# The last feed-forward's output projection by seven block products instead of eight, its modulation tiles moved one feed-forward ahead

## The chip, the cores and the metric

One NeuronCore of a Trainium2 chip runs the whole program in one launch. The metric is the device time of that launch in microseconds (us). The kernel before takes 2341.85 us, the median of three runs (2340.1 to 2344.75).

## The reference

The model is one inference step of a small diffusion backbone: 128 prompt tokens and 512 latent tokens of width 1024 go through two layers. Each layer has a feed-forward, a mixer and a second feed-forward, each with its own shift, scale and gate from a modulation vector. What the change touches is the feed-forward and the modulation:

```python
def ada(cvec, w_mod, b_mod):
    m = jax.nn.silu(cvec) @ w_mod + b_mod          # 9 vectors of 1024: shift, scale, gate three times
    ...
def ffn_sub(x, g, shift, scale, gate, w_in, w_out):
    h = modulate(rms_norm(x, g), shift, scale)
    a, b = jnp.split(h @ w_in, 2, axis=-1)          # 1024 -> 2 x 2816
    return x + gate * (FFN_RESIDUAL * ((jax.nn.silu(a) * b) @ w_out))   # 2816 -> 1024
```

All data are float32. The 2816 inner features are 22 tiles of 128, the 1024 outputs are 8 tiles of 128, and the 640 tokens are two groups of 320.

## The kernel before, in words

**Layout.** Features lie on the 128 partitions and tokens on the free axis. `x` is 8 tiles of 128 x 640. Group 0 holds tokens 0 to 319, all latent; group 1 holds 192 latent and 128 prompt tokens, which have different modulation, so an update of group 1 is two instructions (192 and 128 columns).

**Split operands.** TensorE runs on float32r. Every operand is cut into a high part (ScalarE copies it to float32r, `whi` at L104, `hid` at L583) and a low part (VectorE subtracts, `wlo` at L105, `hid` at L584). A product of two operands is three matmuls: high with high, high with low, low with high. Each matmul has 320 columns.

**A feed-forward** (`ffn`) works through its 22 inner tiles `f`. For each `f` an in-projection makes the tile of `silu(a) * b`, called hidden, which is then split. The first four or five tiles are made with plain products (`in_one`, `start4`). From then on `product_set` (L516) makes the two 1024-deep products of a tile for both token groups as a 2 x 2 block problem with seven block products instead of eight (Strassen's scheme in Winograd's form): VectorE forms sums and differences of the weight halves (L522, L525 to L527), TensorE runs seven products of 12 matmuls each (L126), and ScalarE copies a finished partial sum from one PSUM bank into another (`seeded`, L535) so that the next product accumulates onto it.

**The out-projection** follows in chunks of inner tiles, `CHUNKS = (6, 6, 5, 5)` (L19). A chunk starts when one more hidden tile than it needs is made. For each of the 8 output tiles `m` one weight unit is loaded and split, `mm3` (L128) runs three matmuls for each inner tile and group (L134, L135, L137), and `gate_add` (L400) adds the gated result to `x`. The last chunk goes by halves of four output tiles, each with both groups, and accumulates the squares for the next norm (L294, L298) on its way. In the last feed-forward the final norm (`rstd`, L318, and `final`, L354) and the stores of `yT` follow.

**Modulation.** Layer 0's first vectors are made with TensorE at the start. All later ones are made on VectorE while the feed-forwards run: `mod_tile` (L154) loads a 128 x 1024 piece of the transposed modulation weight into a `raw` buffer and runs two multiply-and-reduce instructions (L159, one per condition vector). `filler` hands such tiles out: four early ones, some spread over the in-projections from `f = 7` on (`spread`, L561), and one after each output tile of the first three chunks. A feed-forward with any of them first loads and activates the condition vectors (`mod_load`, L146). The third feed-forward (layer 1, first) has 36 such tiles, the last one has 4 (L1457, L1462).

**Buffers and order.** Weights come through one DMA queue of SyncE into a ring of 4 `raw` tiles, split weights lie in rings of 5 (`whi`, `wlo`), hidden tiles in a ring of 7, and there are 8 PSUM banks. Every engine runs its own queue in order; a scheduler of the framework lays down that order when the program is built. An instruction whose operand is not ready holds all that stand behind it on its engine.

Of the kernel before, what the change touches and what calls it, by code (L numbers as in the profile page):

```python
# [17 lines left out]
NFT = 22  # L18
CHUNKS = (6, 6, 5, 5)  # L19
# [21 lines left out]
class Body:  # L41
# [58 lines left out]
    def split_w(self, r, n=1024):  # L100
        nc = self.nc
        hi = self.wr.tile([P, 1024], F32R, tag="whi", name=self.nm("whi"))
        lo = self.wr.tile([P, 1024], F32R, tag="wlo", name=self.nm("wlo"))
        a = (nc.scalar.activation(hi[:, :n], r[:, :n], AF.Copy),  # L104
             nc.vector.tensor_tensor(lo[:, :n], r[:, :n], hi[:, :n].bitcast(F32), op=ALU.subtract))  # L105
# [449 lines left out]
    def ffn(self, ctx, l, j, nxt, fill=(), first=False):  # L555
# [3 lines left out]
        nconv = NCONV[2 * l + j]  # L559
        early = 4  # L560
# [9 lines left out]
        def hidden(pa, pb):  # L570
# [7 lines left out]
            return hid_split(sl)  # L578

        def hid_split(sl):  # L580
# [6 lines left out]
        def hidden7(x, z, q, y, w5):  # L587
# [7 lines left out]
            return hid_split(sl)  # L595
# [19 lines left out]
        if first:  # L615
            hid = [hidden(p3[0], p3[1])]
            hid.append(hidden(p3[2], in_one(self.unit(win[l, j, 1, 1]))))
        else:
            self.h_blocks(hp)
            p4 = self.start4([win[l, j, f, ab] for f in range(2) for ab in range(2)], hf=(l, 2 * j))  # L620
            hid = [hidden(p4[0], p4[1]), hidden(p4[2], p4[3])]
# [5 lines left out]
        while len(hid) < nconv:  # L627
# [8 lines left out]
            hid.append(hidden(*p))  # L636
# [4 lines left out]
        def inproj(f):  # L641
            hid.append(hidden7(*self.product_set([win[l, j, f, ab] for ab in range(2)])))
            fill_set(f)

        f0 = 0
        for c, n in enumerate(CHUNKS):
            last = c == len(CHUNKS) - 1
# [5 lines left out]
            if not last:  # L653
# [788 lines left out]
def body(nc, tc, i, o):  # L1442
    with ExitStack() as ctx:
# [73 lines left out]
def layout(a):  # L1517
# [15 lines left out]
    parts, f0 = [], 0  # L1533
    for n in CHUNKS:
        w = a["w_ffn_out"][:, :, f0 * P:(f0 + n) * P].reshape(2, 2, n, P, KT, P)
        parts.append(w.transpose(0, 1, 4, 3, 2, 5).reshape(2, 2, -1))
        f0 += n
    d["w_out"] = np.concatenate(parts, 2)
# [54 lines left out]
```

## Time and profile before

| | |
|---|---|
| median of 3 runs | 2341.85 us |
| profiled execution, its own time | 2340.22 us |
| span of its instructions | 2338.4 us |
| TensorE busy | 2292.8 us, 98% |
| VectorE busy | 1900.8 us, 81% |
| ScalarE busy | 1124.5 us, 48% |
| mean granted TensorE clock | 0.997 of full |

The span runs from the first to the last instruction; the execution's own time is 1.8 us more. The views used below are the page's summary, the chain of work that ended last, lists of who waited for whom, groups of instructions, the DMA list, timelines of one engine and tables of busy time for chosen stretches. In a timeline row stand start, duration, engine, line, operation, output<-input, shapes, and in brackets the idle time before it with what ended it. The last feed-forward fills the stretch from about 1888 us to the end; its first product set starts at 1949.11 us.

### The profile page before, as it was taken

To read this page: it belongs to the slowest core of one execution; us is meant where nothing else is said; L and a number is where in the kernel's file an instruction comes from. 1 tells how busy PE (TensorE), PEld (TensorE's weight loads), DVE (VectorE), ACT (ScalarE), POOL (GpSimd) and SP (SyncE) were. 2 spreads that over 40 slices of the span, in tenths; PEclk is the share of its full clock that TensorE was granted. 3 is DMA by queue.
4 is the path that set the end of the run, shared out by engine and by line. 5 is a ranking of instruction groups with operands and counts; after the bars stand their busy time and mean duration, and the time that the engine had idled before them with its cause. 6 is when DMAs were issued, how large, how long until landed. Compare 5 with 4: busy or idle time off the path is not lost.

```text
span 2338.4 us, 40528 instructions
## 1 busy us (share of the span) xinstructions
PE 2292.8 (98%) x15949; PEld 2220.1 (95%) x15950; DVE 1900.8 (81%) x3779; ACT 1124.5 (48%) x2066; POOL 2.2 (0%) x10
## 2 busy tenths in 40 slices
PE   9999999999999999999999999999999999999998
PEld 6999999998889999999999999998888899999997
DVE  6999989795889989787888888969878798565665
ACT  5535253463666434334552525347756674252442
POOL 0000000000000000000000000000000000000000
PEclk9999999999999999999999999999999999999999
DMA  7353544332111535343234343422100013222221
GB/s 295 118 189 125 192 136 162 111 108 89 47 48 64 169 111 162 100 155 126 82 113 160 108 159 113 147 94 79 42 29 28 28 54 122 78 90 75 89 72 64
DMA packets 81230, 253.31 MB, mean 108 GB/s; under 512 B 9616, under 2 KB 15632, under 8 KB 81040
## 3 DMA queue, kind: packets, MB, share of 16 engines
q1 hardware_dynamic: 81040, 250.72, 32.4%
q8 instruction: 126, 2.06, 0.4%
q14 instruction: 64, 0.52, 0.1%
HBM read 247.28 MB, written 3.41 MB: 107 GB/s over the span
## 4 chain that ended last, share of the span: by engine, by line
PE 87%; DVE 7%; ACT 2%; DMA 2%; issue 1%; SPq 0%; DVEq 0%; ACTq 0%
PE mm L126 34%; PE mm L134 15%; PE mm L135 15%; PE mm L137 15%; PE tr L730 2%; PE pv L1368 2%; PE sc L1333 1%; DVE wlo L105 1%; DMA rawm<-in_wmT 1%; PE pv L1133 1%; DVE t L298 1%; DVE x L400 1%; DVE s L1337 1%; PE mm L881 0%; DVE junk L159 0%
## 5 line engine op out<-in xcount | busy, mean ns | idle before, releaser
L104 ACT ACTIVATE whi<-raw 128x1024 fp32r<-128x1024 f32 (+2 forms) x419 | 407.2, 978 | 564.9 <-PE mm L135 255.5
L105 DVE TENSOR_TENSOR wlo<-raw,whi 128x1024 fp32r<-128x1024 f32 (+2 forms) x419 | 465.6, 1116 | 113.1 <-ACT whi L104 112.6
L134 PE MATMUL mm<-hid,whi 128*128 128x320 f32 x1408 | 427.3, 310 | 0.0
L135 PE MATMUL mm<-hid,whi 128*128 128x320 f32 x1408 | 425.7, 308 | 0.0
L126 PE MATMUL mm<-hhi,whi 128*128 128x320 f32 x1136 | 351.0, 309 | 0.0
L126 PE MATMUL mm<-hhi,wlo 128*128 128x320 f32 x1136 | 350.8, 309 | 0.0
L126 PE MATMUL mm<-hlo,whi 128*128 128x320 f32 x1136 | 350.4, 308 | 0.0
L137 PE MATMUL mm<-hid,wlo 128*128 128x320 f32 x1408 | 346.2, 309 | 0.0
L159 DVE CUSTOM_DVE_ANT_0 junk<-rawm,sil 128x1024 bf16<-128x1024 f32 x256 | 312.0, 1219 | 22.5 <-DMA rawm<-in_wmT 17.6
L400 DVE SCALAR_TENSOR_TENSOR x<-mm,mod,x 128x192 f32<-128x192 f32 (+2 forms) x576 | 226.2, 433 | 114.0 <-PE mm L137 112.7
L134 PE MATMUL mm<-hhi,whi 128*128 128x320 f32 x896 | 276.3, 320 | 6.2 <-ACT hhi L345 5.6
L135 PE MATMUL mm<-hlo,whi 128*128 128x320 f32 x896 | 274.9, 312 | 0.7 <-DVE hlo L348 0.6
L135 PEld LDWEIGHTS mm<-hid,whi 128*128 128x128 f32 x1408 | 264.3, 188 | 0.8
L134 PEld LDWEIGHTS mm<-hid,whi 128*128 128x128 f32 x1408 | 264.3, 188 | 0.8
L137 PE MATMUL mm<-hhi,wlo 128*128 128x320 f32 x896 | 247.9, 311 | 2.8 <-DVE wlo L105 2.8
L137 PEld LDWEIGHTS mm<-hid,wlo 128*128 128x128 f32 x1408 | 241.4, 188 | 0.0
L126 PEld LDWEIGHTS mm<-hhi,whi 128*128 128x128 f32 x1136 | 213.2, 188 | 0.1
L126 PEld LDWEIGHTS mm<-hlo,whi 128*128 128x128 f32 x1136 | 213.3, 188 | 0.0
L126 PEld LDWEIGHTS mm<-hhi,wlo 128*128 128x128 f32 x1136 | 213.2, 188 | 0.0
L134 PEld LDWEIGHTS mm<-hhi,whi 128*128 128x128 f32 x896 | 167.3, 189 | 15.0 <-ACT hhi L345 8.7
L126 PE MATMUL mm<-Th,whi 128*128 128x320 f32 x568 | 175.7, 309 | 3.0 <-ACT mm L535 3.0
L126 PE MATMUL mm<-Tl,whi 128*128 128x320 f32 x568 | 175.2, 308 | 0.0
(229 smaller groups left out, 4094.6 us busy)
## 6 DMA issues: line engine op xcount, KB each, us to landing
raw<-in_w_in SPq DMA_DIRECT2D x176, 512.0 KB, 3.8
rawm<-in_wmT SPq DMA_DIRECT2D x128, 512.0 KB, 3.7
raw<-in_w_out SPq DMA_DIRECT2D x64, 384.0 KB, 3.5
raw<-in_w_out SPq DMA_DIRECT2D x64, 320.0 KB, 3.0
wm<-in_wm SPq DMA_DIRECT2D x16, 512.0 KB, 10.2
raw<-in_w_ab SPq DMA_DIRECT2D x12, 512.0 KB, 4.2
raw<-in_w_c SPq DMA_DIRECT2D x10, 512.0 KB, 3.6
sil<-in_c SPq DMA_DIRECT2D x8, 512.0 KB, 4.8
```

The lines of the kernel that those rows point to most:

```text
L104: a = (nc.scalar.activation(hi[:, :n], r[:, :n], AF.Copy), nc.vector.tensor_tensor(lo[:, :n], r[:, :n], hi[:, :n].bitcast(F32), op=ALU.sub ...
L105: nc.vector.tensor_tensor(lo[:, :n], r[:, :n], hi[:, :n].bitcast(F32), op=ALU.subtract))
L126: nc.tensor.matmul(out, a[:, c], b, start=start and first, stop=last, skip_group_check=True)
L134: nc.tensor.matmul(out, hi[:, c], rh, start=start, stop=False)
L135: nc.tensor.matmul(out, hi[:, c], rl, start=False, stop=False)
L137: nc.tensor.matmul(out, lo[:, c], rh, start=False, stop=stop)
L159: nc.vector.tensor_tensor_reduce(out=self.junk, in0=r, in1=self.sil[:, q], op0=ALU.mult, op1=ALU.add, scale=1.0, scalar=0.0, accum_out=sel ...
L298: t = nc.vector.tensor_tensor(a, a, sq, op=ALU.add)
L400: a = nc.vector.scalar_tensor_tensor(out=x[:, c], in0=ps[:, c], scalar=self.mod[:, q, l, v, m:m + 1], in1=x[:, c], op0=ALU.mult, op1=ALU.add)
L730: self.nc.tensor.transpose(ps[:, a * P:(a + 1) * P], src[:, b * P:(b + 1) * P], self.ident)
L1133: nc.tensor.matmul(st["pv"][64 * f:64 * f + 64, ti * P:(ti + 1) * P], V[:, sl, vc[f]], st[ti, f][:, a * P:(a + 1) * P], start=a == 0, stop ...
L1368: nc.tensor.matmul(st["pv"][64 * f:64 * f + 64, ti * P:(ti + 1) * P], V[:, (4, 0, 1, 2, 3)[a], vc], rhs, start=a == 0, stop=a == 4)
```

## The change

Only the last feed-forward (layer 1, second) computes its out-projection differently.

- Its chunks become 4, 4, 4, 4 and 6 inner tiles. The chunks of four use a new function `out_set`; the last chunk of six keeps the old form.
- `out_set` makes two output tiles at a time. The four inner tiles, as two halves of two, the two output tiles and the two token groups are a 2 x 2 block problem, done with seven products of 6 matmuls (L690 in the new program) instead of eight. VectorE forms four 128 x 256 combinations of the two weight tiles (L676 to L679). Three of the products need combinations of hidden tiles.
- `hid_split` prepares those: of the first two tiles of a chunk only group 0 is split (`hk`, a new ring of three), and the rest is kept unsplit until the tile two places on is there; then three differences are taken (L599 to L601) and three full splits are made instead of one.
- The four sets of a chunk are interleaved in the code: four steps of one set alternate with the first three of the next.
- The four modulation tiles of the last feed-forward move into the third, which then has 40; `mod_begin` and the loading of the condition vectors drop out of the last.
- The output weight is laid out to match; for the other three feed-forwards the chunks stay.

```diff
-CHUNKS = (6, 6, 5, 5)
+CHUNKS = ((6, 6, 5, 5),) * 3 + ((4, 4, 4, 4, 6),)
+SEVEN = 3
...
-        def hid_split(sl):
+        def hid_split(sl, f):
+            if not seven or f >= NFT - chunks[-1]:
+                return split_full(sl)
+            k = f % 4
+            b11, b12 = grp(sl, 0), grp(sl, 1)
+            if k < 2:
+                half = hp.tile([P, 2, G], F32R, tag="hk", bufs=3, name=self.nm("hk"))
+                nc.scalar.activation(half[:, 0], b11, AF.Copy)
+                nc.vector.tensor_tensor(half[:, 1], b11, half[:, 0].bitcast(F32), op=ALU.subtract)
+                nc.vector.tensor_tensor(b11, b12, b11, op=ALU.subtract)
+                kept[f] = sl
+                return half[:, 0], half[:, 1]
+            h2 = split_full(sl)
+            t = kept.pop(f - 2)
+            t1, t3, t4, t2 = grp(t, 0), grp(t, 1), b11, b12
+            nc.vector.tensor_tensor(t3, b12, t3, op=ALU.subtract)
+            nc.vector.tensor_tensor(t2, b12, t1, op=ALU.subtract)
+            nc.vector.tensor_tensor(t4, b11, t2, op=ALU.subtract)
+            pairs[f] = h2, split_full(t), split_full(sl)
+            return h2
...
+        def out_set(wa, wb, m, f0):
+            half = lambda t, a, b=None: t[:, 256 * a:256 * (a + 1 if b is None else b)]
+            r, s = (self.raw.tile([P, 1024], F32, tag="raw", name=self.nm("raw")) for _ in range(2))
+            nc.sync.dma_start(out=half(r, 0, 2), in_=wb)
+            nc.sync.dma_start(out=half(r, 2, 4), in_=wa)
+            nc.vector.tensor_tensor(half(s, 0), half(r, 0), half(r, 1), op=ALU.add)
+            nc.vector.tensor_tensor(half(s, 1), half(s, 0), half(r, 2), op=ALU.subtract)
+            nc.vector.tensor_tensor(half(s, 2), half(r, 2), half(r, 0), op=ALU.subtract)
+            nc.vector.tensor_tensor(half(s, 3), half(r, 3), half(s, 1), op=ALU.subtract)
+            wr = self.split_w(r, slice(256, 1024))
+            ws = self.split_w(s)
...
+            x = self.bank()[:, :G]
+            product(x, wr, 2, h1, True)
+            yield
+            w = self.bank()[:, :G]
+            product(w, ws, 0, side(t13, 0), True)
+            y = seeded(x)
+            w5 = self.g()
+            nc.scalar.activation(w5, w, AF.Copy)
+            yield
+            product(y, ws, 1, side(t42, 1), False)
+            z = seeded(y)
+            yield
+            product(x, wr, 3, side(hh, 0), False)
+            self.gate_add(m, 0, x, l, v)
+            yield
+            product(y, ws, 2, side(t13, 1), False)
+            q = seeded(y)
+            t = self.g()
+            nc.vector.tensor_tensor(t, y, w5, op=ALU.add)
+            self.gate_add(m + 1, 1, t, l, v)
+            yield
+            product(z, ws, 3, side(hh, 1), False)
+            nc.vector.tensor_tensor(w5, z, w5, op=ALU.add)
+            self.gate_add(m, 1, w5, l, v)
+            yield
+            product(q, wr, 1, side(t42, 0), False)
+            self.gate_add(m + 1, 0, q, l, v)
+            yield
...
+            if seven and not last:
+                behind = None
+                for m in range(0, KT, 2):
+                    step = out_set(wc[m], wc[m + 1], m, f0)
+                    for k in range(3):
+                        if behind:
+                            next(behind)
+                        next(step)
+                    if behind:
+                        next(behind)
+                    behind = step
+                for _ in behind:
+                    pass
...
-            b.ffn(c, 1, 0, (1, 1), vf(1, range(4, 9))[:36])
+            b.ffn(c, 1, 0, (1, 1), vf(1, range(4, 9)))
...
-            b.mod_begin(c)
-            b.ffn(c, 1, 1, None, vf(1, range(4, 9))[36:])
+            b.ffn(c, 1, 1, None)
```

Three places show how the queues look. The numbers in the names tell tiles apart. In the new program the line numbers are a little higher: its L107 is the old L105 (`wlo`), its L402 the old L400 (`gate_add`), its L524, L527 to L529 the old L522, L525 to L527, its L161 the old L159.

The first is VectorE in the out-projection's first chunk of the last feed-forward. Before, it stood so (two output tiles):

```order
L400 SCALAR_TENSOR_TENSOR x_70<-mm_22123,mod,x_70 128x320
L400 SCALAR_TENSOR_TENSOR x_70<-mm_22124,mod,x_70 128x192
L400 SCALAR_TENSOR_TENSOR x_70<-mm_22124,mod,x_70 128x128
L105 TENSOR_TENSOR wlo_22355<-raw_22352,whi_22354 128x768
L400 SCALAR_TENSOR_TENSOR x_71<-mm_22170,mod,x_71 128x320
L400 SCALAR_TENSOR_TENSOR x_71<-mm_22171,mod,x_71 128x192
L400 SCALAR_TENSOR_TENSOR x_71<-mm_22171,mod,x_71 128x128
L105 TENSOR_TENSOR wlo_22402<-raw_22399,whi_22401 128x768
```

Now a stretch of it reads as follows; `wlo_22009` and `wlo_22082`, just ahead of it, belong to the third and the fourth set of the chunk, and `raw_22180` is a weight of the next in-projection.

```order
L715 TENSOR_TENSOR g_22027<-mm_21961,g_21963 128x320
L402 SCALAR_TENSOR_TENSOR x_73<-g_22027,mod,x_73 128x192
L402 SCALAR_TENSOR_TENSOR x_73<-g_22027,mod,x_73 128x128
L524 TENSOR_TENSOR s_3632_22182<-raw_22180 128x512
L719 TENSOR_TENSOR g_21963<-mm_21980,g_21963 128x320
L527 TENSOR_TENSOR raw_22180<-raw_22178,raw_22180 128x512
L402 SCALAR_TENSOR_TENSOR x_72<-g_21963,mod,x_72 128x192
L402 SCALAR_TENSOR_TENSOR x_72<-g_21963,mod,x_72 128x128
L402 SCALAR_TENSOR_TENSOR x_73<-mm_22025,mod,x_73 128x320
L107 TENSOR_TENSOR wlo_22086<-raw_22074,whi_22085 128x1024
```

The last row is the low part of the fourth set's combined weights. It now stands behind two instructions (L524, L527) that read the next in-projection's weight.

The second is TensorE in the same chunk. Before, the first rows of one output tile (its first inner tile, both groups):

```order
L134 MATMUL mm_22217<-hid_21429,whi_22213 128x320
L135 MATMUL mm_22217<-hid_21429,whi_22213 128x320
L134 MATMUL mm_22218<-hid_21429,whi_22213 128x320
L135 MATMUL mm_22218<-hid_21429,whi_22213 128x320
L137 MATMUL mm_22217<-hid_21429,wlo_22214 128x320
L137 MATMUL mm_22218<-hid_21429,wlo_22214 128x320
```

Now, where the fourth set's second product begins (`mm_22108`, weights `whi_22085` and `wlo_22086`), between the first matmul of the third set's sixth product (`mm_22057`) and the rest of it:

```order
L690 MATMUL mm_22057<-hid_21585,whi_22008 128x320
L690 MATMUL mm_22108<-hid_21591,whi_22085 128x320 x2
L690 MATMUL mm_22108<-hid_21591,wlo_22086 128x320
L690 MATMUL mm_22108<-hid_21725,whi_22085 128x320 x2
L690 MATMUL mm_22108<-hid_21725,wlo_22086 128x320
L690 MATMUL mm_22057<-hid_21585,whi_22008 128x320
```

The matmul on `wlo_22086` is the third of its product; all products behind it on TensorE wait with it.

The third is VectorE in the third feed-forward, at the in-projection of `f = 7`. Before:

```order
L525 TENSOR_TENSOR raw_14189<-raw_14187,raw_14189 128x512
L105 TENSOR_TENSOR wlo_14075<-raw_14055,whi_14074 128x1024
L590 TENSOR_TENSOR g_14043<-mm_14000,g_14002 128x320
L592 TENSOR_TENSOR g_14002<-mm_13974,g_14002 128x320
L105 TENSOR_TENSOR wlo_14194<-raw_14187,whi_14193 128x1024
```

Now:

```order
L527 TENSOR_TENSOR raw_14189<-raw_14187,raw_14189 128x512
L161 ISA junk,mod<-rawm_14317,sil 128x1024
L161 ISA mod 128x1
L161 ISA junk,mod<-rawm_14317,sil 128x1024
L161 ISA mod 128x1
L107 TENSOR_TENSOR wlo_14075<-raw_14055,whi_14074 128x1024
L615 TENSOR_TENSOR g_14043<-mm_14000,g_14002 128x320
```

One modulation tile (two multiply-and-reduce instructions, each with a read of its sum) has been put ahead of a weight split; three more stand further on.

More of the change, by code (lines that the diff above doesn't have):

```diff
@@ L559, in ffn @@
         nconv = NCONV[2 * l + j]
+        chunks, seven = CHUNKS[2 * l + j], 2 * l + j == SEVEN
+        pairs, kept = {}, {}
         early = 4
@@ L568, in ffn, with hidden @@
         v = 2 + 6 * j
-        def hidden(pa, pb):
+        def hidden(f, pa, pb):
             sl = self.t()
@@ L585, in hid_split, with hidden7 @@
             return hi, lo
-        def hidden7(x, z, q, y, w5):
+        def hidden7(f, x, z, q, y, w5):
             sl, t = self.t(), self.g()
@@ L615, in ffn @@
         if first:
-            hid = [hidden(p3[0], p3[1])]
-            hid.append(hidden(p3[2], in_one(self.unit(win[l, j, 1, 1]))))
+            hid = [hidden(0, p3[0], p3[1])]
+            hid.append(hidden(1, p3[2], in_one(self.unit(win[l, j, 1, 1]))))
         else:
@@ L620, in ffn @@
             p4 = self.start4([win[l, j, f, ab] for f in range(2) for ab in range(2)], hf=(l, 2 * j))
-            hid = [hidden(p4[0], p4[1]), hidden(p4[2], p4[3])]
+            hid = [hidden(f, p4[2 * f], p4[2 * f + 1]) for f in range(2)]
         if fill:
@@ L635, in ffn @@
                 p.append(in_one(w))
-            hid.append(hidden(*p))
+            hid.append(hidden(len(hid), *p))
         for _ in sums:
@@ L641, in inproj, with product, seeded @@
         def inproj(f):
-            hid.append(hidden7(*self.product_set([win[l, j, f, ab] for ab in range(2)])))
+            hid.append(hidden7(f, *self.product_set([win[l, j, f, ab] for ab in range(2)])))
             fill_set(f)
+        def out_set(wa, wb, m, f0):
[9 more added lines that the diff above has]
+            ws = self.split_w(s)
+            h1 = [hid[f0 + k] for k in range(2)]
+            hh, t13, t42 = zip(*(pairs[f0 + k] for k in (2, 3)))
+            side = lambda t, g: [(grp(a, g), grp(b, g)) for a, b in t]
+            def product(p, w, j, rs, start):
+                for k, (rh, rl) in enumerate(rs):
+                    c = slice((2 * j + k) * P, (2 * j + k + 1) * P)
+                    for a, b, first, last in ((w[0], rh, k == 0, False), (w[0], rl, False, False), (w[1], rh, False, k == 1)):
+                        nc.tensor.matmul(p, a[:, c], b, start=start and first, stop=last, skip_group_check=True)
+            def seeded(src):
+                p = self.bank()[:, :G]
+                nc.scalar.activation(p, src, AF.Copy)
+                return p
+            x = self.bank()[:, :G]
[26 more added lines that the diff above has]
+            yield
@@ L645, in ffn @@
         f0 = 0
-        for c, n in enumerate(CHUNKS):
-            last = c == len(CHUNKS) - 1
+        for c, n in enumerate(chunks):
+            last = c == len(chunks) - 1
             while len(hid) < min(NFT, f0 + n + 1):
@@ L652, in ffn @@
             hk = lambda k, g: (grp(ht[k][0], g), grp(ht[k][1], g))
-            if not last:
+            if seven and not last:
[11 more added lines that the diff above has]
+                    pass
+            elif not last:
                 for m in range(KT):
```

23 lines of the change are left out of this document (13 added, 10 removed).

## The prediction, made before the changed kernel was run

> **What bounds the kernel now.** I read the page's summary first, then for the stretch that changes the chain that ended last, TensorE's waits and the tables of busy time.
>
> ```profile
> PE 2292.8 (98%) x15949; PEld 2220.1 (95%) x15950; DVE 1900.8 (81%) x3779; ACT 1124.5 (48%) x2066; POOL 2.2 (0%) x10
> 1949.11 36.92 PE mm L126 x252
> 2028.27 73.83 PE mm L126 x504
> 2144.35 61.53 PE mm L126 x420
> 2241.07 49.22 PE mm L126 x336
> ```
>
> The last four rows are the chain's long pieces in the last feed-forward: uninterrupted TensorE work, at 73.83 / 504 = 0.1465 us for each 320-column matmul. One in-projection (84 matmuls) is 12.3 us.
>
> ```profile
> PE mm L137 <- DVE wlo L105: 0.4, 1, 0.4
> 1929.20:1987.60 58.40, 58.40 (x400) 58.40 (x399) 47.38 (x75) 27.55 (x46) 0.00 (x0) 1.00 0.38 122
> 1987.60:2104.60 117.00, 117.00 (x801) 117.00 (x800) 73.20 (x112) 47.31 (x75) 0.00 (x0) 1.00 0.25 84
> 2104.60:2280.00 175.40, 175.40 (x1198) 175.40 (x1198) 109.66 (x174) 67.87 (x106) 0.00 (x0) 1.00 0.24 79
> ```
>
> The first row is TensorE's only wait from 1899 to 2322 us. The others give, after the length of the stretch, busy time of TensorE, its weight loads, VectorE and ScalarE. TensorE is never idle, the granted clock is 1.00, and VectorE is busy 73.20 of 117.00 us, 63%. So a matmul taken out of this stretch is 0.1465 us off the end, as long as VectorE can feed the new form.
>
> **Removed: 96 matmuls.** Plain, 22 inner tiles x 8 output tiles x 2 groups x 3 = 1056 matmuls. Now 4 chunks x 4 sets x 7 products x 6 = 672, and the last chunk 6 x 8 x 2 x 3 = 288: 960. The gain is 96 x 0.1465 = **14.06 us**. It is on the path, since nothing else ended last there.
>
> **Moved: four modulation tiles.** Each is one 512 KB load and two L159 instructions.
>
> ```profile
> L159 DVE CUSTOM_DVE_ANT_0 junk<-rawm,sil 128x1024 bf16<-128x1024 f32 x256 | 312.0, 1219 | 22.5 <-DMA rawm<-in_wmT 17.6
> 1220.00:1280.00 60.00, 58.92 (x402) 58.66 (x402) 53.93 (x96) 18.39 (x27) 0.00 (x0) 1.00 0.54 178
> 1340.00:1400.00 60.00, 60.00 (x411) 60.00 (x410) 52.54 (x93) 17.70 (x25) 0.00 (x0) 1.00 0.53 169
> PE mm L126 <- ACT mm L535: 1.4, 2, 1.1
> ```
>
> That is 2 x 1.22 = 2.4 us of VectorE each, in in-projections of 12.3 us in the third feed-forward, where VectorE has about 7 us in 60 free (rows two and three) and DMA is busy half the time. Twelve of fifteen in-projections carry one such tile instead of eight. I cost it at nothing, because TensorE's work covers it. The bound from above is the first feed-forward, which spreads 20 tiles over the same fifteen in-projections: the last row is TensorE's whole wait there from 100 to 470 us, 1.4 us. So 0 to 1.4 us. In the last feed-forward the four tiles with their loads, the two loads of condition vectors and their activation go from a stretch in which TensorE never waited, so nothing is gained on the path; but eight L159 instructions (9.8 us of VectorE's 47.38 in the first table row) make room for what follows.
>
> **Added: VectorE work.** Prices come from neighbours in its timeline:
>
> ```profile
> 2036.34 1.23 DVE L105 TENSOR_TENSOR wlo<-raw,whi 128x1024 fp32r<-128x1024 f32 x1 [1.85 <-ACT whi L104]
> 2038.85 0.49 DVE L590 TENSOR_TENSOR g<-mm,g 128x320 f32<-128x320 f32 x1 [1.29 <-PE mm L126]
> 2039.45 0.49 DVE L592 TENSOR_TENSOR g<-mm,g 128x320 f32<-128x320 f32 x1
> 2039.86 1.22 DVE L105 TENSOR_TENSOR wlo<-raw,whi 128x1024 fp32r<-128x1024 f32 x1
> 2040.99 0.48 DVE L593 TENSOR_TENSOR t<-t,mm 128x320 f32<-128x320 f32 x1
> 2041.39 0.48 DVE L594 TENSOR_TENSOR t<-t,g 128x320 f32<-128x320 f32 x1
> 2041.79 0.68 DVE L526 TENSOR_TENSOR raw<-s,raw 128x512 f32<-128x512 f32 x1
> 2042.51 0.69 DVE L527 TENSOR_TENSOR raw<-raw 128x512 f32<-128x512 f32 x1
> 2043.11 0.82 DVE L584 TENSOR_TENSOR hid<-t,hid 128x640 fp32r<-128x640 f32 x1
> 2101.39 0.95 DVE L105 TENSOR_TENSOR wlo<-raw,whi 128x768 fp32r<-128x768 f32 x1
> 2102.26 0.48 DVE L593 TENSOR_TENSOR t<-t,mm 128x320 f32<-128x320 f32 x1
> 1991.21 1.14 DVE L400 SCALAR_TENSOR_TENSOR x<-mm,mod,x 128x320 f32<-128x320 f32 x3 [2.51 <-PE mm L137]
> 1992.26 0.95 DVE L105 TENSOR_TENSOR wlo<-raw,whi 128x768 fp32r<-128x768 f32 x1
> ```
>
> From start to start an instruction costs about 0.08 us less than its own duration: 1.14 for 1024 columns, 0.87 for 768, 0.74 for 640 (0.82 less 0.08), 0.60 for 512, 0.40 for 320, 1.05 for the three gate updates of an output tile, of which the 320-column one is 0.46 and the pair 0.59. Where the next instruction depends on it, 0.11 to 0.12 us more (2038.85 to 2039.45, 2041.79 to 2042.51). No row has 256 columns; the line through 320 and 512 gives 0.33, an estimate, and the bounds are 0.30 (half the gate pair of 192 and 128) and 0.40 (320 columns), so a chunk's sixteen could be 0.5 us cheaper or 1.1 dearer.
>
> A set is then 4 x 0.33 + 0.87 + 1.14 + 2 x 0.40 + 2 x 1.05 = 6.2 us of VectorE beside 42 x 0.1465 = 6.15 us of TensorE. Four sets are 25 us beside 24.6. Four in-projections are 4 x (5 x 0.60 + 3 x 1.14 + 4 x 0.40) = 32.1, and their hidden tiles 2 x 0.80 + 2 x (3 x 0.40 + 3 x 0.74) = 8.4. A chunk has 65.5 us on VectorE, 69 with some 30 dependences, beside 4 x 12.3 + 24.6 = 73.8 on TensorE. ScalarE gains per set four bank copies (0.42 each) and two splits of at most 1.06, under 3.8 us beside 6.15, and four more hidden splits a chunk; it was busy 47.31 of 117.00, so that is covered. The loads keep their bytes; two of 256 KB a set take the place of two whole ones. The chunk fits on VectorE, at 93%, but the out-projection alone does not: half its splits must be done ahead, and the order does that (five of eight).
>
> **Where a wait appears.** I walk one out-projection stage by the new order, in TensorE slots of 6 x 0.1465 = 0.879 us. More rows for it: hand-over from TensorE to ScalarE, ScalarE's split, and loads.
>
> ```profile
> 2033.24 0.31 PE L126 MATMUL mm<-Th,wlo 128*128 128x320 f32 x1
> 2033.58 0.42 ACT L535 ACTIVATE mm<-mm 128x320 f32<-128x320 f32 x1 [0.95 <-PE mm L126]
> 2035.24 1.06 ACT L104 ACTIVATE whi<-raw 128x1024 fp32r<-128x1024 f32 x1 [1.23 <-PE mm L126]
> raw<-in_w_in SPq DMA_DIRECT2D x35, 512.0 KB, 3.6
> DMA to landing us min/median/max: 3.4/3.8/5.8
> ```
>
> A product's last matmul ends 0.31 us after its start, 0.17 into the next slot, and its reader starts 0.03 later; a bank copy is 0.42. A seed has one slot of cover at worst (first set: 0.20 + 0.42 against 0.88), so seeds cost nothing, up to 0.1 us each.
>
> The third set's combined split `wlo_22009` must reuse the slot of the first set's `wr`, free after that set's seventh product, the tenth slot: 8.8 + 0.2 = 9.0. ScalarE's half ends at 10.1, VectorE's at 11.3. It is wanted at 11.9: no wait. But this split also frees the `raw` tile into which the next in-projection's second weight goes, so that load is issued at 11.4 and lands 3.6 later, at 15.0. VectorE goes on with two gates (0.92), `wlo_22082` (0.87) and the second set's L715 with its gates (1.2) to 14.2 and then stands at L524 until 15.0. Behind it come L524 itself (0.60), L719, L527, a gate pair and a gate (0.41 + 0.60 + 0.59 + 0.46), so `wlo_22086` starts at 17.7 and ends at 18.9. TensorE wants it with the third matmul of the product shown in the second place, after twenty slots and three matmuls, at 18.0. **TensorE stands about 1.0 us.** After that VectorE has 9.4 us of gates, sums and the next weights ahead of the split of the next in-projection's third product, which is ready at 29.4; TensorE wants it at 24.6 + 1.0 + 3.5 + 0.3 = 29.4: 0 to 0.2 us. I take 1.2 us for each of four chunks, 4.8 us. In the four in-projections behind it VectorE catches up, so lateness is not carried over: 32.1 + 8.4, plus the sums and five splits done ahead (4 x 4 x 0.33 + 2 x 2.01 + 0.87 = 10.2), less the 4.1 of weights that the stage has already done, is 46.6 of 49.2. Below, the cost is nothing if the load lands 1 us earlier; above, a load of 5.8 us (last row, the slowest in the first feed-forward) adds 2.2.
>
> [...] The rows above overlap neighbours by 0.08 us. [...]
>
> **The end.**
>
> ```profile
> 2325.96 0.31 PE L137 MATMUL mm<-hid,wlo 128*128 128x320 f32 x1
> 2326.67 0.66 DVE L400 SCALAR_TENSOR_TENSOR x<-mm,mod,x 128x192 f32<-128x192 f32 x2
> 2327.25 1.00 DVE L354 SCALAR_TENSOR_TENSOR x<-x,gn,t 128x320 f32<-128x320 f32 x2
> ```
>
> The last gate starts 0.40 us after the last matmul ended, because VectorE is behind. With 18 instead of 15 matmuls for a tile, TensorE's last four tiles take 4 x 3 x 0.1465 = 1.8 us longer and VectorE is not behind: 0.4 us gained (0 to 0.7).
>
> **Sum.** 2340.22 - 14.06 + 4.8 - 0.4 = 2330.6 us for an execution like the profiled one. The median of the runs lies 1.6 us above that execution: **2332 us**, 10 us or 0.4% less.
>
> **Rivals.**
>
> *Nothing waits* (0.20). If the load lands by 14 us of the stage, VectorE never stands and 2341.85 - 14.06 - 0.4 = 2327.4. For it: 0.8 us of 3.6 decides. Against it: no such chunk has slack on VectorE.
>
> *The stand at the load is long* (0.18). At 5.8 us landing each chunk loses 1.2 + 2.2 = 3.4 us, 13.6 in all: 2341, the same as before. For it: 5.8 occurred. Against it: DMA is busy only 0.25 and 0.24 in the last two table rows, and these loads go out one at a time.
>
> *VectorE sets the pace of the whole chunk* (0.10, the other side). Place: the four chunks of the last feed-forward. If every one of about 120 instructions costs its full duration, 65.5 becomes 75.1; 30 dependences at 0.11 make it 78.4; the stands of a queue in order that the walk shows (8.4 to 10.1 for ScalarE's half, 14.2 to 15.0 for the load) 80.9. Against 73.8 that is 7.1 a chunk: 2327.4 + 28.4 = 2356, slower. It decides from 73.8 + 14.5 / 4 = 77.4 us a chunk on. For it: 93% leaves little. Against it: the overlap in the rows.
>
> That the change does not do what it says is excluded: the new order holds 15226 matmuls, the old 15322.
>
> **How the numbers follow.** The forecast has 0.52. Its own range is 2329 to 2337 (0.5 to 2 us a chunk, and the third feed-forward's 1.4). The range for 8 in 10 takes in the case without waits and most of the long stand: 2326.5 to 2341. A measurement of this kernel can tell about 0.2% (4.7 us) from no change. Faster by more than that: 0.52 + 0.20 = 0.72; the same: 0.18; slower: 0.10.
>
> **What would show it.** In the new profile TensorE has 96 matmuls fewer; its waits in the last feed-forward are some 4 to 5 us, on `wlo` at L107 from the product line L690, four of about 1 us; L524 waits for its load once a chunk. No new wait of TensorE in the third feed-forward. Wrong if TensorE waits on bank copies, if waits lie in the in-projections, or if the four chunks take more than 77 us each.

## The result and the profile after

The changed kernel takes 2327.2 us (median of 2326.5 to 2330.1) beside 2341.1 us for the kernel before, measured together: a ratio of 0.994, with a 95% interval of 0.992 to 0.996. A second, later comparison gave 2328.5 beside 2342.5, 0.995 (0.993 to 0.996). The forecast was 2332 us, so it had the direction and the gain of the removed matmuls, and one term too much: the 4.8 us of standing still.

The profiled execution of the changed kernel took 2330.1 us, span 2328.4 us. TensorE's long pieces from the chain that ended last, in the last feed-forward, with L690 the seven products and L128 the in-projections (start, length, what, number of matmuls):

```profile
1952.47 12.31 PE mm L128 x84
1964.77 22.89 PE mm L690 x156
2039.14 22.89 PE mm L690 x156
2113.55 24.64 PE mm L690 x168
2138.19 49.23 PE mm L128 x336
2187.42 24.76 PE mm L690 x168
2212.18 61.68 PE mm L128 x420
```

A stage of 168 matmuls lasts 24.64 us, 0.1467 us each, which is the rate of a plain stretch (49.23 / 336 = 0.1465). The two rows with 156 are cut by the chain's path and not by a stop. The next fence is the table of TensorE's waits from 1880 to 2310 us, with what it waited for, the us in total, how often, and the longest:

```profile
PE mm L136 <- ACT hhi L347: 2.2, 1, 2.2
PE mm L137 <- DVE hlo L350: 0.8, 3, 0.4
PE mm L128 <- ACT mm L537: 0.5, 2, 0.3
PE mm L139 <- DVE wlo L107: 0.4, 1, 0.4
```

The first two rows belong to the beginning of the feed-forward; the wait of the last one stood there before. **No row has L690:** the table names no wait of TensorE in the new stages. (The fourth stage, with 24.76 us, is 0.12 us over the others all the same.) The table of busy time by stretch says how close VectorE is (length, TensorE, weight loads, VectorE, ScalarE; then granted clock and DMA):

```profile
1964.77:1989.39 24.62, 24.62 (x170) 24.62 (x169) 22.55 (x47) 13.30 (x25) 0.00 (x0) 1.00 0.27 86
1989.39:2039.14 49.75, 49.52 (x339) 49.26 (x338) 44.53 (x75) 29.48 (x49) 0.00 (x0) 1.00 0.26 86
2138.19:2187.42 49.23, 49.23 (x339) 49.23 (x338) 44.53 (x75) 29.35 (x49) 0.00 (x0) 1.00 0.26 86
```

A chunk has 22.55 + 44.53 = 67.1 us of VectorE beside 74.4 us, 90%. The second row also shows a small loss that the forecast didn't have: the four in-projections behind the first stage (and those behind the second) take 49.75 us instead of the 49.23 of the third row. In the second profile of the change the first three stretches take 49.63, 49.85 and 49.40 us. The chain that ended last leaves TensorE there. Three of its pieces in the first stretch, and the wait on VectorE at the end of the load:

```profile
1991.27 2.28 DVE wlo L107 x2
1993.57 4.38 DMA raw<-in_w_in
2009.27 3.77 DMA raw<-in_w_out
```

```profile
1997.97 0.69 DVE L524 TENSOR_TENSOR s<-raw 128x512 f32<-128x512 f32 x1 [0.64 <-DMA raw<-in_w_in]
```

Two weight splits free a `raw` tile, a load into it lands 4.38 us later, VectorE has waited for it, and a second load stands behind that work.

**Where the time went.** From the first product set of the last feed-forward to the end of the span the kernel before takes 2338.4 - 1949.11 = 389.29 us and the changed one 2328.4 - 1952.47 = 375.93 (375.84 in a second profile). That is 13.36 us less. Removed matmuls give 14.06. The end, with its last chunk of six, gives 0.65 (a run below has it without the products). Against them stand 1.3 us: twice 0.52 in the in-projections just shown, 0.12 in the fourth stage (24.76) and 0.15 behind it (61.68 for 420 matmuls, 61.53 at full rate). 14.06 + 0.65 - 1.3 = 13.4.

The whole spans differ by 10.0 us only, since the profiled execution of the changed kernel lost time in a place that the change doesn't touch: in the second mixer the granted clock was lower. The same two stretches of 20 us, first of before, then of after:

```profile
1620.00:1640.00 20.00, 16.16 (x118) 14.43 (x119) 19.79 (x51) 15.33 (x28) 0.00 (x0) 1.00 0.33 113
1640.00:1660.00 20.00, 17.00 (x146) 14.15 (x145) 17.17 (x51) 18.12 (x45) 0.00 (x0) 1.00 0.17 57
```

```profile
1620.00:1640.00 20.00, 16.85 (x114) 15.11 (x113) 19.26 (x50) 14.76 (x28) 0.00 (x0) 0.91 0.35 113
1640.00:1660.00 20.00, 17.02 (x118) 14.12 (x116) 14.73 (x44) 16.05 (x39) 0.00 (x0) 0.83 0.17 57
```

In the second stretch 118 matmuls were done instead of 146, at a clock of 0.83 instead of 1.00. In that profile the clock stood at 0.50 from 1628.9 to 1632.3 and from 1649.4 to 1656.2 us; the last section comes back to it. That is why the last feed-forward is compared from its own start.

### The profile page after: what moved, and what is told of

Read it like the earlier page. It is cut to its first block, busy times and chain, and to the rows that moved or that the text cites. A ratio compares the mean times of both kernels' runs of the same rounds, so it can differ in the third digit from the quotient of the medians.

```text
span 2328.4 us, 40561 instructions
## 1 busy us (share of the span) xinstructions
PE 2282.6 (98%) x15854; PEld 2207.7 (95%) x15854; DVE 1973.6 (85%) x3955; ACT 1166.6 (50%) x2153; POOL 2.2 (0%) x10
## 4 chain that ended last, share of the span: by engine, by line
PE 81%; DVE 12%; ACT 3%; DMA 3%; issue 2%; SPq 0%; DVEq 0%; ACTq 0%
PE mm L128 30%; PE mm L136 13%; PE mm L137 12%; PE mm L139 12%; PE mm L690 4%; DVE wlo L107 2%; PE tr L824 2%; PE pv L1462 2%; DVE junk L161 1%; DMA rawm<-in_wmT 1%; PE sc L1427 1%; DVE x L402 1%; DVE g L344 1%; DVE hlo L350 1%; PE pv L1227 1%
## 5 line engine op out<-in xcount | busy, mean ns | idle before, releaser
L106 ACT ACTIVATE whi<-raw 128x1024 fp32r<-128x1024 f32 (+2 forms) x427 | 417.6, 986 | 461.1 <-PE mm L137 174.3
L107 DVE TENSOR_TENSOR wlo<-raw,whi 128x1024 fp32r<-128x1024 f32 (+2 forms) x427 | 479.7, 1130 | 74.8 <-ACT whi L106 74.0
L128 PE MATMUL mm<-hhi,whi 128*128 128x320 f32 x1136 | 350.9, 309 | 0.0
L128 PE MATMUL mm<-hhi,wlo 128*128 128x320 f32 x1136 | 350.9, 309 | 0.0
L128 PE MATMUL mm<-hlo,whi 128*128 128x320 f32 x1136 | 350.5, 309 | 0.0
L136 PE MATMUL mm<-hid,whi 128*128 128x320 f32 x1152 | 350.2, 310 | 0.0
L137 PE MATMUL mm<-hid,whi 128*128 128x320 f32 x1152 | 349.0, 309 | 0.0
L161 DVE CUSTOM_DVE_ANT_0 junk<-rawm,sil 128x1024 bf16<-128x1024 f32 x256 | 312.4, 1221 | 24.7 <-DMA rawm<-in_wmT 19.9
L139 PE MATMUL mm<-hid,wlo 128*128 128x320 f32 x1152 | 289.2, 309 | 0.0
L402 DVE SCALAR_TENSOR_TENSOR x<-mm,mod,x 128x320 f32<-128x320 f32 (+2 forms) x536 | 216.0, 440 | 65.9 <-PE mm L139 64.5
L137 PEld LDWEIGHTS mm<-hid,whi 128*128 128x128 f32 x1152 | 216.2, 188 | 0.7
L136 PEld LDWEIGHTS mm<-hid,whi 128*128 128x128 f32 x1152 | 216.2, 188 | 0.7
L128 PEld LDWEIGHTS mm<-hlo,whi 128*128 128x128 f32 x1136 | 213.3, 188 | 0.0
L128 PEld LDWEIGHTS mm<-hhi,wlo 128*128 128x128 f32 x1136 | 213.3, 188 | 0.0
L128 PEld LDWEIGHTS mm<-hhi,whi 128*128 128x128 f32 x1136 | 213.2, 188 | 0.0
L139 PEld LDWEIGHTS mm<-hid,wlo 128*128 128x128 f32 x1152 | 199.2, 188 | 0.0
L128 PE MATMUL mm<-Th,whi 128*128 128x320 f32 x568 | 176.1, 310 | 3.0 <-ACT mm L537 3.0
L128 PE MATMUL mm<-Th,wlo 128*128 128x320 f32 x568 | 175.3, 309 | 0.0
```

Source lines behind the costliest of these rows:

```text
L106: a = (nc.scalar.activation(hi[:, c], r[:, c], AF.Copy), nc.vector.tensor_tensor(lo[:, c], r[:, c], hi[:, c].bitcast(F32), op=ALU.subtract))
L107: nc.vector.tensor_tensor(lo[:, c], r[:, c], hi[:, c].bitcast(F32), op=ALU.subtract))
L128: nc.tensor.matmul(out, a[:, c], b, start=start and first, stop=last, skip_group_check=True)
L136: nc.tensor.matmul(out, hi[:, c], rh, start=start, stop=False)
L137: nc.tensor.matmul(out, hi[:, c], rl, start=False, stop=False)
L139: nc.tensor.matmul(out, lo[:, c], rh, start=False, stop=stop)
```

## The experiments

The questions were: are the removed matmuls the whole gain, does the moved modulation cost anything, why did TensorE not stand, and how much room was left on VectorE and on the load.

### One part alone: the chunks without the products, and the move by itself

```diff
-SEVEN = 3
+SEVEN = -1
```

> The change with its chunks of 4, 4, 4, 4 and 6 and its moved modulation, but with every output tile of the last feed-forward computed plainly: 96 matmuls more, none of the sums, copies and combined splits. Theory (the whole gain is the removed matmuls, at 0.1465 us each, with nothing lost beside them): 2327.2 + 14.06 = 2341.3 us, and no wait of TensorE in the last feed-forward. Rival (a part of the gain is from the other chunking or from the modulation that has left this feed-forward): clearly under 2339 us.

Measured: 2340.7 us, 0.9995 of before (0.9986 to 1.0004). From the first product set to the end the trace has 2338.4 - 1949.76 = 388.64 us: 0.65 less than before, which is what the last chunk of six gives, and 12.7 to 12.8 more than the change, 14.06 less the 1.3 of small waits. So the products give the gain, but for the 0.65 of the end.

The modulation alone, in the kernel before:

```diff
-CHUNKS = ((6, 6, 5, 5),) * 3 + ((4, 4, 4, 4, 6),)
-SEVEN = 3
+CHUNKS = ((6, 6, 5, 5),) * 4
+SEVEN = -1
```

> The kernel before with one part of the change: the four modulation tiles moved from the last feed-forward into the third, all else plain in chunks of 6, 6, 5 and 5. Theory (VectorE's free time covers them in the third feed-forward, and nothing waited for them in the last): 2341.1 us, within 0.5 us. Rival (the bound from the first feed-forward): 1.4 us more, 2342.5. Other rival (their absence is worth something in the last feed-forward): under 2339.

Measured: 2341.9 us beside 2341.8, 1.0002 (0.9993 to 1.0011). TensorE's waits in the third feed-forward with all 40 tiles, among those from 1150 to 1640 us:

```profile
PE mm L139 <- DVE wlo L107: 1.4, 1, 1.4
PE mm L128 <- ACT mm L537: 1.0, 1, 1.0
```

The kernel before has 1.4 and 1.3 us there. The move is free, as costed. (Its profiled last feed-forward is 0.75 us longer than that of the kernel before, 2341.1 - 1951.06 = 390.04 us beside 389.29. At least 0.6 of it lies in the last two matmuls, which ran at half the clock; the last section shows them.)

### Why there was no stand: the slot

In the first stage of the change, ScalarE's half of the third set's combined split (its first row below), VectorE's half, L524 and the fourth set's split:

```profile
1971.70 1.06 ACT L106 ACTIVATE whi<-raw 128x1024 fp32r<-128x1024 f32 x1
```

```profile
1972.97 1.22 DVE L107 TENSOR_TENSOR wlo<-raw,whi 128x1024 fp32r<-128x1024 f32 x1
...
1977.83 0.69 DVE L524 TENSOR_TENSOR s<-raw 128x512 f32<-128x512 f32 x1
1978.43 0.48 DVE L719 TENSOR_TENSOR g<-mm,g 128x320 f32<-128x320 f32 x1
...
1980.48 1.22 DVE L107 TENSOR_TENSOR wlo<-raw,whi 128x1024 fp32r<-128x1024 f32 x1
```

The split begins 1971.70 - 1964.77 = 6.9 us into the stage, and not 9.0. The prediction took the slots in a strict rotation. The built program gives the third set's combined split the address of the first set's *combined* split, which is read last in the sixth product, and not that of its `wr`, which the seventh still reads. So everything behind it is some 2 us earlier: the load is there when L524 comes up at 13.06 us of the stage (no idle time stands in its row), and the fourth set's split ends at 16.9.

To test this, the split was made to wait for the seventh product:

```diff
             ws = self.split_w(s)
+            if sevenths:
+                self.tc.add_manual_dep(self.last_split.ins, sevenths[-1].ins.name, mybir.DependencyInfo(
+                    mybir.DependencyClass.Sync, mybir.DependencyReason.DATA), reason="ring")
...
-            product(q, wr, 1, side(t42, 0), False)
+            sevenths.append(product(q, wr, 1, side(t42, 0), False))
```

> The change, with the combined split of the third and of the fourth set made to wait for the seventh product of the first and of the second set, as the prediction had assumed, where the trace of the change shows it begin after the sixth product, 6.9 us after the stage's start. The scheduler knows of the wait and puts L524 two groups of gates later. Theory (the slot sets when the load is issued): ScalarE's half begins at about 9.0 us of the stage, the next in-projection's second weight is issued at 11.3 and lands at about 15.0, the fourth set's split ends at 17.7 instead of 16.9, still just before the 18.0 at which TensorE wants it: 0 to 0.5 us a chunk, 2327 to 2329. The walk of the prediction, with the order as it was, gives 1.0 to 1.2 us a chunk, 2332. Rival (the slot doesn't matter for the load): the load is issued at 9.5 us of the stage as before and the time is 2327.2.

Measured: 2326.3 us, 0.9931 (0.9918 to 0.9943). The first stage starts at 1961.57 here. ScalarE's half, then L524 and the splits behind it on VectorE, then the chain:

```profile
1970.40 1.80 ACT L106 ACTIVATE whi<-raw 128x1024 fp32r<-128x1024 f32 x2 [0.40 <-PE mm L695]
```

```profile
1976.47 0.69 DVE L524 TENSOR_TENSOR s<-raw 128x512 f32<-128x512 f32 x1 [0.40 <-DMA raw<-in_w_in]
1977.08 1.00 DVE L402 SCALAR_TENSOR_TENSOR x<-mm,mod,x 128x320 f32<-128x320 f32 x2
1978.00 2.35 DVE L107 TENSOR_TENSOR wlo<-raw,whi 128x1024 fp32r<-128x1024 f32 x2
```

```profile
1961.57 24.64 PE mm L695 x168
1986.21 49.23 PE mm L128 x336
2035.44 24.64 PE mm L695 x168
2060.08 49.23 PE mm L128 x336
```

The split now begins at 8.8 us of the stage (9.0 was walked), L524 at 14.9, held by its load (15.0), and the fourth set's split ends at 1978.00 + 1.22, 17.65 (17.7). The times of the walk come out, and still TensorE doesn't stand. The reason is the order: the scheduler, which knows when the slot comes free, moved L524 behind one more sum with its gates, so that only two gates lie between it and the fourth set's split. The walk had combined a late slot with an order that had been made for an early one. This kernel also loses nothing in its in-projections (49.23 us): its last feed-forward takes 2323.9 - 1949.26 = 374.64 us, 1.2 to 1.3 less than the change. Its total time can't be told from the change's, as the intervals overlap.

### What a late load would cost

The mechanism of the forecast was that L524 heads VectorE's queue and the fourth set's split stands behind it. To delay the load alone, an unrelated transfer was started beside it in each of the four stages, on GpSimd's queue; the order on the other engines stays the same. In the diff, `split[4]` is ScalarE's half of the third set's combined split:

```diff
         def inproj(f):
+            if seven and f in (5, 9, 13, 17):
+                d = more.tile([2, P, D], F32, tag="more", name=self.nm("more"))
+                a = nc.gpsimd.dma_start(out=d, in_=win[l, j, 0:2, 0])
+                self.tc.add_manual_dep(a.ins, split[4].ins.name, mybir.DependencyInfo(
+                    mybir.DependencyClass.Sync, mybir.DependencyReason.DATA), reason="beside")
```

> The change, with one extra transfer of 1 MB from memory to memory in each of the four stages, started on another queue when ScalarE has done its half of the third set's combined split, about 8 us into the stage, so that it runs beside the load that L524 waits for. The order of instructions on every engine stays the same. Theory (L524 heads VectorE's queue, and the fourth set's split is behind it): each us by which L524 starts later than 13.06 us of the stage delays that split by as much, and beyond a margin of 1.1 us TensorE stands for it. With an estimate of 6 us instead of 3.6 for the load's landing that is 15.5 - 13.06 - 1.1 = 1.3 us a chunk, 5 us in all: 2332; and whatever the landing is, the stand on the fourth set's wlo is L524's start less 14.2. Rival (the margin is larger, or VectorE works off the delay): 2327 to 2328 and no stand on wlo of L690.

Measured: 2403.6 us, 1.026 (1.025 to 1.028), 15 times the expected loss. The transfer took far longer than estimated, and the load with it. The issue row of the transfer (its last number is the time to landing), L524 in the first stage, and TensorE's stand:

```profile
more<-in_w_in POOLq DMA_DIRECT2D x1, 23.2
```

```profile
1996.12 0.69 DVE L524 TENSOR_TENSOR s<-raw 128x512 f32<-128x512 f32 x1 [18.61 <-DMA raw<-in_w_in]
```

```profile
1997.85 0.90 PE L699 MATMUL mm<-hid,whi 128*128 128x320 f32 x2 [16.76 <-ACT mm L703]
```

The place was wrong too: with so long a delay TensorE stands at a bank copy before it gets to the fourth set's split, since a sum behind L524 has to free the bank. The next run kept everything but the size, 256 KB in rows of 2 KB:

```diff
-                d = more.tile([2, P, D], F32, tag="more", name=self.nm("more"))
-                a = nc.gpsimd.dma_start(out=d, in_=win[l, j, 0:2, 0])
+                d = more.tile([P, 512], F32, tag="more", name=self.nm("more"))
+                a = nc.gpsimd.dma_start(out=d, in_=win[l, j, 0, 0][:, :512])
```

> As the run with 1 MB beside the load, with 256 KB in its place, in rows of 2 KB. The 1 MB took 23.2 us and held L524 until 31.75 us of the first stage, 18.7 us late; TensorE stood 16.8 us at a bank copy. A quarter of that size is estimated to hold L524 for 2 to 5 us. Theory (the fourth set's split is behind L524 with a margin of 1.1 us): the stage grows by L524's delay d beyond 13.06 us, less 1.1, so 1 to 4 us a chunk, 4 to 16 in all, 2331 to 2343, and for each stage the trace shows stage length = 24.64 + d - 1.1. Rival (only a very long delay reaches TensorE, since VectorE or other buffers absorb several us): 2327 to 2329 although d is 2 us or more.

Measured: 2330.7 us, 0.9952 (0.9939 to 0.9964), with L524 late by 0 to 1.1 us instead of 2 to 5. Its last feed-forward takes 2327.7 - 1951.55 = 376.15 us, 0.2 to 0.3 more than the change; the rest of the 2 to 3 us between the medians isn't explained, and the intervals of the two overlap. Two runs with larger pieces filled the gap:

```diff
-                d = more.tile([2, P, D], F32, tag="more", name=self.nm("more"))
-                a = nc.gpsimd.dma_start(out=d, in_=win[l, j, 0:2, 0])
+                d = more.tile([32, 3840], F32, tag="more", name=self.nm("more"))
+                a = nc.gpsimd.dma_start(out=d, in_=win[l, j, 0, 0].rearrange("(a b) d -> a (b d)", b=4)[:, :3840])
```

> As the runs with a transfer beside the load, to get a delay between the 0.3 us of 256 KB in rows of 2 KB and the 18.7 us of 1 MB in pieces of 64 KB: 480 KB in 32 rows of 15 KB. Theory: a stage in which L524 starts d later than 13.06 us is 24.64 + d - 1.1 us long if d is over 1.1, and 24.64 if it is not; below d = 2 the stand is on the fourth set's wlo, above it TensorE stands first at a bank copy, because L719 behind L524 frees the bank. With d of 3 to 8 us by the sizes, 8 to 28 us in all: 2335 to 2355. Rival (VectorE or the buffers absorb several us): the stage is longer by clearly less than d - 1.1.

Measured: 2332.0 us, 0.9959 (0.9946 to 0.9971), on one chip with the change itself at 2328.5.

> The same with 448 KB in 64 rows of 7 KB. Theory as for the rows of 15 KB, with a smaller d, by the sizes 0.5 to 4 us: 2327 to 2339, and in every stage the length is 24.64 us up to d = 1.1 and d - 1.1 more above it. Rival: the stage grows with d from nothing on (no margin), or not at all up to several us.

(In its diff the piece is `[64, 1792]` with `b=2`.) Measured: 2331.0 us, 0.9956 (0.9943 to 0.9968).

> The change itself, on the same chip as the two runs with a transfer beside the load, so that they have it to be compared with. Every theory: 2327.2 us, 0.994 of the time before; the four stages 24.6 to 24.8 us long, L524 of the next in-projection at 13.1 to 14.0 us of each.

Measured: 2328.5 us, 0.9946 (0.9932 to 0.9959), and L524 at 13.05 to 13.11 us in all four stages.

In the run with rows of 15 KB, TensorE's waits from 1945 to 2250 us, and the fourth stage (it starts at 2187.67) on VectorE and TensorE:

```profile
PE mm L128 <- ACT mm L537: 2.2, 3, 1.0
PE mm L699 <- DVE wlo L107: 0.9, 2, 0.6
```

```profile
2202.45 0.69 DVE L524 TENSOR_TENSOR s<-raw 128x512 f32<-128x512 f32 x1 [1.64 <-DMA raw<-in_w_in]
```

```profile
2206.38 0.42 PE L699 MATMUL mm<-hid,wlo 128*128 128x320 f32 x1 [0.61 <-DVE wlo L107]
2213.09 0.31 PE L128 MATMUL mm<-hhi,whi 128*128 128x320 f32 x1
```

This is the stand that the forecast described, at the place it named: L524 waits for its load, and the product line for `wlo`. The stages of the four kernels, each by when L524 starts in it and when the first matmul of the next in-projection starts (2202.45 - 2187.67 and 2213.09 - 2187.67 in the rows above; 24.47 where nothing waits):

| Stage of | L524 starts, us of the stage | next in-projection, us of the stage | longer by |
|---|---|---|---|
| change, second profile, all four | 13.05 to 13.11 | 24.47 to 24.48 | 0 |
| 256 KB, 2 KB rows: 1st, 2nd, 3rd | 13.33, 13.45, 13.05 | 24.47 | 0 |
| 7 KB rows, 1st | 13.69 | 24.47 | 0 |
| 7 KB rows, 4th | 13.94 | 24.58 | 0.11 |
| change, first profile, 4th | 13.96 | 24.60 | 0.13 |
| 256 KB, 4th, and 7 KB rows, 2nd | 14.14 | 24.78 | 0.31 |
| 15 KB rows, 3rd | 14.15 | 24.80 | 0.33 |
| 15 KB rows, 1st | 14.20 | 24.83 | 0.36 |
| 7 KB rows, 3rd | 14.33 | 24.97 | 0.50 |
| 15 KB rows, 2nd | 14.35 | 25.00 | 0.53 |
| 15 KB rows, 4th | 14.78 | 25.42 | 0.95 |
| 1 MB, 1st | 31.75 | 42.77 | 18.30 |

Up to 13.83 us nothing is lost, and behind it each us of L524's delay is a us of the stage (14.78 - 13.83 = 0.95). So the mechanism is as walked. (The last row, where TensorE stood at another place and came back at half its clock, lies 0.4 us above the line.) The margin is 13.83 - 13.06 = 0.77 us instead of the 1.1 of the expectations, and the rival with more room falls. For L524 at the prediction's 15.0 us the line gives 1.17 us a stage, beside 1.0 in the walk: about the right price for a load that landed at 15.0 under this order. It landed before 13.1 in seven of the eight stages profiled, and in the eighth at 13.96.

The table holds the stages alone. With the rows of 15 KB the whole last feed-forward takes 2330.3 - 1949.43 = 380.87 us, 5.0 more than the change's 375.84. The stages account for 2.2 of it; 2.7 lie in the in-projections behind them, where TensorE waits for the bank copy L537 (first row of the fence above). (They take 3.9 us more than at full rate, 1.2 in the change.) So VectorE doesn't make up the lateness there, which the prediction took it to do.

### How much room VectorE has

More instructions of 256 columns behind each in-projection (four; in the second run eight):

```diff
             nc.vector.tensor_tensor(grp(sl, 1), grp(sl, 1), w5, op=ALU.mult)
+            if seven:
+                for _ in range(4):
+                    nc.vector.tensor_tensor(self.cst[:, 0:256], sl[:, :256], sl[:, :256], op=ALU.add)
```

> The change, with four more VectorE instructions of 256 columns, 0.33 us each from start to start, behind each in-projection from the fifth on in the last feed-forward (they read the new hidden tile and write constants that are no longer used): 5.3 us more on VectorE for each four in-projections. Theory (a chunk of stage and four in-projections has 67.1 us of VectorE beside 74.4 of TensorE, so 72.4 still fits): 0 to 3 us in all, 2327 to 2330. Rival (VectorE already sets the pace, the whole chunk being waits in a chain): nearly all of it comes out at the end, up to 18 x 1.33 = 24 us, 2345 to 2351.

Measured: 2326.8 us, 0.9938 (0.9926 to 0.9951). The first two chunks:

```profile
1962.13:2035.99 73.86, 73.86 (x507) 73.86 (x506) 71.39 (x135) 42.57 (x73) 0.00 (x0) 1.00 0.27 83
2035.99:2109.86 73.87, 73.87 (x507) 73.87 (x506) 72.45 (x137) 42.44 (x73) 0.00 (x0) 1.00 0.28 87
```

> The same with eight instructions: 10.6 us more a chunk, 77.7 of VectorE beside 74.4. Theory: 3.3 us over for each of four chunks, 13 us, and some stands of the queue beside it: 2340 to 2345, so the whole gain is gone, and VectorE is busy nearly all of the time from the first stage on. Rival (short instructions cost their full 0.42 us with nothing overlapped): 67.1 + 13.4 = 80.5, 6.1 us over, 24 in all, 2351.

Measured: 2342.9 us, 1.0005 of before (0.9996 to 1.0014). The first chunk, and the start of the second:

```profile
1962.66:2036.71 74.05, 74.05 (x507) 73.88 (x506) 73.14 (x144) 41.26 (x71) 0.00 (x0) 1.00 0.25 79
2036.71:2110.00 73.29, 71.11 (x471) 68.93 (x471) 71.17 (x142) 39.00 (x67) 0.00 (x0) 1.00 0.25 80
```

Five us more are free, with VectorE busy 72.45 of 73.87 us, 98%, and TensorE without a gap. Ten us more take the whole gain: from the first product set to the end 2340.6 - 1950.35 = 390.25 us, 14.3 more than the change, where the sum of start-to-start prices gives 13. Of the other 1.3, 0.6 lie at the end, where the last two matmuls took 1.43 us instead of 0.81; the rest isn't explained. The rival in which each instruction costs its full 0.42 us would have given 24.

### The interleaving

```diff
                 for m in range(0, KT, 2):
                     step = out_set(wc[m], wc[m + 1], m, f0)
-                    for k in range(3):
-                        if behind:
-                            next(behind)
-                        next(step)
-                    if behind:
-                        next(behind)
-                    behind = step
-                for _ in behind:
-                    pass
+                    for _ in step:
+                        pass
```

> The change with the sets of output tiles one after the other instead of two interleaved. Theory (a seed is copied in 0.20 + 0.42 us and has one product of 0.88 us to do it in; no product waits): no change, 2327.2 within 1.5 us, and no wait of TensorE on bank copies. Rival (the interleaving is what hides the copies): three seeds in each of sixteen sets, 0.2 to 0.5 us each, 10 to 24 us, 2337 to 2351.

Measured: 2328.5 us, 0.9943 (0.993 to 0.9957), and the table of TensorE's waits from 1950 to 2300 us is empty. The copies of seeds don't need the second set; one product covers each. The rival falls.

## Why the prediction was right or wrong

The measured 2327.2 us lies below the forecast's own range of 2329 to 2337. The range for 8 in 10 holds it only because it took in the case without waits, which had a chance of 0.20. The direction and the gain were worked out; that nothing stands was not.

- **What bounds the kernel, and the price of a removed matmul: right.** 96 x 0.1465 = 14.06 us is the difference between plain and new stages (12.7 to 12.8, and 1.3 of small waits); the new stages run at 0.1467 us a matmul. The late-slot run, whose stages and in-projections have none of these waits, has it whole: 388.64 - 374.64 = 14.0.
- **The moved modulation: right.** 0 of the 0 to 1.4, by the run that moves it alone.
- **VectorE's price: right.** 65.5 to 69 us a chunk were forecast, 67.1 measured. The 256-column instruction starts 0.33 us before the next (1968.80 to 1969.13 in the first stage), the value taken. One reading was off: L592 at 2039.45 starts 0.60 us behind L590, so 0.20 and not 0.11 above the price of 0.40; the chunk's sum did not suffer.
- **Seeds for nothing: right**, even without the interleaving.
- **The end: right within its range** (0 to 0.7): 0.65 where 0.4 stood.
- **The stand of TensorE, 1.2 us for each of four chunks, 4.8 in all: wrong, 0.1 us measured in the stages.** The step that failed is "must reuse the slot of the first set's `wr` ..., free after that set's seventh product". The split took another slot, free after the sixth, began at 6.9 and not 9.0 us, and its load was no longer late for L524. The price that was put on the delay was about right (1.17 by the table for the 1.0 of the walk), its cause was absent. The run with the late slot shows that the step failed in a second way: with that slot the scheduler would have written another order, and TensorE would not have stood either.
- **A loss that was not foreseen:** about 0.5 us in each of the first two stretches of in-projections; the table of waits names the bank copy L537 for 0.5 us of the two together. The late-slot run and the run with four more instructions, which have other orders, don't have it; the run with one set at a time has it in the first stretch only. The chain there runs through two weight splits, the load that waits for their `raw` tile (4.38 us) and VectorE's work behind it, so it is again a load that comes late for L524, but in the in-projections. The prediction had put lateness there at nothing, since VectorE catches up. No run isolates that load.
- **The rivals.** What happened is the first, "nothing waits", 2327.4. The long stand at the load (5.8 us landing) didn't occur. The point from which VectorE would decide, 77.4 us a chunk, holds: 67.1 + 10.6 = 77.7 us gave the time of the kernel before to 0.1%. Neighbouring instructions overlap as the rows said: the added short instructions cost 14.3 us and not the 24 of full durations.

## What to carry to other kernels

A wait that rests on which buffer comes free first must be read from the built program, by addresses or by the first row that shows the release; a ring of five tiles need not go round in order. An order made by a scheduler already contains the releases that it counts on, so if the walk finds a load late by two us for an instruction that the scheduler put there, the walk's release is the first thing to doubt. And a busy share is no margin by itself: at 98% VectorE cost nothing here, while 0.8 us of delay in one load was all the room that the stage had.

## What was not expected of the hardware

**Large pieces of one transfer held up a load on another queue.** 480 KB in rows of 15 KB took 3.7 us to land and put L524 back by 1.1 to 1.7 us; 1 MB in pieces of 64 KB took 23.2 us and put it back by 18.7. The issue row of the run with 15 KB rows:

```profile
more<-in_w_in POOLq DMA_DIRECT2D x4, 480.0 KB, 3.7
```

The DMA records of the 1 MB run show how. In its first stage the 1 MB went as sixteen pieces of 64 KB, two at a time and one pair behind the other, 2.42 us for most of them. Between one piece and the next came a single 4 KB packet of the load that L524 waits for, 0.16 us: a piece at 1980.02, a packet at 1982.43, a piece at 1982.59, a packet at 1985.00, and so on to the last pieces, which ended at 1995.28 and 1995.43. L524 started at 1996.12. In the other runs a piece of 15 KB took 0.77 us in the median, and one of 7 KB 0.30. Bytes and piece size were changed together between the runs, so the share of each wasn't isolated.

**After the stand of 16.8 us TensorE came back at half its clock.** The first 2.83 us after it, and what followed:

```profile
1997.85:2000.68 2.83, 2.83 (x10) 2.83 (x11) 2.83 (x6) 1.67 (x3) 0.00 (x0) 0.50 0.00 0
2000.68:2006.00 5.32, 5.32 (x38) 5.32 (x38) 5.32 (x12) 1.28 (x3) 0.00 (x0) 1.00 0.32 99
```

Ten matmuls in 2.83 us at a granted clock of 0.50, then 1.00; behind the stands of the other three stages it took 5.2, 2.8 and 6.0 us. The first stage was 18.30 us longer, 1.5 us more than its stand of 16.76: ten matmuls at 0.1465 us would have taken 1.47 us and not 2.83. Behind the stands of 0.25 and 0.61 us in the run with rows of 15 KB the matmuls started 0.15 us apart again from the second on, so these stands didn't lower the clock.

**Stands of 1.9 to 2.6 us halved it in some executions.** It didn't happen every time. The last two matmuls of the kernel before, and those of the run that only moves the modulation, behind the same stand (last bracket):

```profile
2328.71 0.81 PE L314 MATMUL mm<-t,cst 128*128 128x320 f32 x2 [2.44 <-DVE t L298]
```

```profile
2330.67 1.44 PE L316 MATMUL mm<-t,cst 128*128 128x320 f32 x2 [2.45 <-DVE t L300]
```

The granted clock was 1.00 in the first and 0.50 in the second. In the change and in the run with four more VectorE instructions that stand is 1.93 us, and the two matmuls behind it took 0.81 and 1.33 us. The stand of 2.55 us in the second mixer is the same in both profiles of the result section; behind it the clock was 1.00 in the kernel before and 0.50 in the changed one. So part of the difference between two executions comes from whether the clock falls at such a stand, and that has to be looked for when two profiles are compared.
